# Sparse-attention scores: low query part over all 128 rows with zero-padded keys, compressed keys of both groups in one tile

## The chip, the cores and the metric

The kernel runs on one core of one Trainium2 chip. The metric is the device time of one execution in microseconds (us), the median of three runs. Engines are named as in the profile: PE is TensorE's matmul stream and PEld its weight loads, DVE is VectorE, ACT is ScalarE, POOL is GpSimd, SP issues the DMAs.

## The reference

The program is four transformer layers on 256 tokens of width 1024, all in fp32. The change is in the first, whose mixer has two halves: retention (4 heads) and sparse attention (8 query heads in 2 groups of 4, 64 wide), joined and projected. Sparse attention adds three branches with gates:

```python
s_c = einsum('bghqd,bgnd->bghqn', qb, k_cmp) * scale     # 15 compressed keys for each group
p_c = masked_softmax(s_c, cmp_end[None, :] <= t[:, None])
...
s_s = einsum('bghqd,bgqkd->bghqk', qb, kg) * scale       # chosen blocks of keys
s_w = einsum('bghqd,bgkd->bghqk', qb, kw) * scale        # a window of keys
return gb[0] * o_c + gb[1] * o_s + gb[2] * o_w
```

`k_cmp` comes from a small network over blocks of 32 tokens. With 256 tokens there are four blocks of 64 and up to eight may be chosen, and the window is 512, so both the s and the w branch see every earlier key: they are two plain causal attentions with keys of their own, ks and kw. A head j of both groups g is handled together.

## The kernel before

All weights pass through `weights` (L235): a DMA on SP brings 128x1024 fp32 into `raw`, ScalarE makes a rounded high part `hi` (L240), VectorE the rest `lo` (L243). A projection (`proj_fm`, `mm3`) makes for each of 8 slices three matmuls with 256 columns, high times high, high times low, low times high (L248 to L250). `proj_tm` (L284 to L286) does the same with 512 columns and tokens as rows. Both write PSUM banks of a pool of three, `pa`.

`even_mixer` projects in this order: the keys and values for compression, the sparse values, the queries `nq` (two pairs of tiles, L755), the keys ks and kw (L768), then the retention queries and keys rq and rk (two pairs each, L871 and L872), values rv (L873), and gates (L908). Instructions are put on the five engines in an order that is planned at build time: the program's order sets their priority, and an instruction whose operands and buffer are there can be put ahead of one that waits. On the chip each engine then works strictly in that order.

The queries: group 0 lies in rows 0 to 63, group 1 in rows 64 to 127 of `nq`. For each group a tile `qq` holds the high part of the query twice, in both halves of the rows (L762, L763), and `ql` holds the low part, group g in its own 64 rows (L764). The keys: `ksw[g]` holds the high part of ks and kw of the group in the group's own rows (L774) and the low part in the other rows (L775). The scores of head j, group g, are two matmuls, one over 128 rows (high query against high and low keys, L823) and one over the group's 64 rows (low query against high keys, L824), 512 columns for the second half of the tokens (t = 1) and 256 for the first. VectorE masks them and takes the minimum (L826), ScalarE the exponential (L833), VectorE scales (L841), PE transposes (L844 to L846), ScalarE copies (L848), and PE multiplies by the values (L861).

The compressed keys of both groups lie in `kcm`, 128 rows by 16 columns, group g in its rows (L738). Their scores are sixteen fp32 matmuls over 64 rows with 16 columns, into a bank for each group (L783). An fp32 matmul is two instructions with two weight loads in the trace. VectorE adds the mask, once for each bank (L787).

Buffers: `big` (L264) gives out tiles of 128x512 from a pool of 13. vsw, qq, ql, ksw, the three tables (L606, L869), rope (L611), the parts rqh, rql, rkh, rkl (L595), rv and rg all come from it. `rope_pair` takes a projection out of its bank: ScalarE copies with halves exchanged (L589, L590), VectorE multiplies by the two halves of rope (L592, L593) and adds (L594), in tiles of the pool `ev` (four buffers), then the split into high and low (L596, L597). At the end `out_proj` takes the four sparse heads and the four retention heads.

Of the kernel before, what the change touches and what calls it, by code (L numbers as in the profile page):

```python
# [9 lines left out]
F32 = mybir.dt.float32  # L10
F32R = mybir.dt.float32r
AF = mybir.ActivationFunctionType
ALU = mybir.AluOpType
# [155 lines left out]
def _model(es, tc, I, out):  # L169
    nc = tc.nc  # L170
    V, A, T, G = nc.vector, nc.scalar, nc.tensor, nc.gpsimd

    def pool(name, bufs, **kw):
        return es.enter_context(tc.tile_pool(name=name, bufs=bufs, **kw))

    cst = pool("cst", 1)
# [28 lines left out]
    def C(name):  # L205
        o, n = _COFF[name]
        return cs[:, o - 128:o - 128 + n]
# [50 lines left out]
    def att(tag, shape=(128, 512)):  # L258
        if tag == "sc":
            turn[0] ^= 1  # L260
            tag = f"s{turn[0]}"
        return pt.tile(list(shape), F32, tag=tag, name=tag, bufs=PB[tag])

    def big(name="b", dt=F32):  # L264
        return bp.tile([128, 2, S], dt, tag="big", name=name)
# [116 lines left out]
    def two(ap, n=2):  # L382
        return ap.unsqueeze(1).to_broadcast([128, n, S])
# [198 lines left out]
    def transpose_to(ps, src):  # L582
        T.transpose(ps, src, ident)  # L583
# [64 lines left out]
    def late_constants():  # L648
        nc.sync.dma_start(out=vg, in_=I["vec"])
        nc.sync.dma_start(out=lt, in_=I["lam"])  # L650
        V.tensor_copy(lmask, C("levmask")[:, 0:NLEV * 32].rearrange("p (l c) -> p l c", l=NLEV))
        for a in hat:
            G.memset(a, 0.0)
        le = cst.tile([128, 8], F32, name="le")
        lg = vg[:, V_LB:V_LB + 8]
        V.tensor_tensor(out=le, in0=lg, in1=lg, op=ALU.subtract)
        A.activation(le, le, AF.Exp)
        V.reciprocal(lb, le)
        V.tensor_tensor(out=lb, in0=lb, in1=le, op=ALU.mult)
        V.tensor_tensor(out=lb, in0=lb, in1=lb, op=ALU.subtract)  # L660
        V.tensor_scalar(out=lb, in0=lb, scalar1=0.0, scalar2=None, op0=ALU.max)
        V.tensor_scalar(out=om, in0=lb, scalar1=-1.0, scalar2=1.0, op0=ALU.mult, op1=ALU.add)
        for i in range(3):
            for j, o in enumerate((V_LNG, V_LNB)):
                c = vg[:, o + 8 * i:o + 8 * i + 8]
                A.activation(gbs[0][:, i, :, j], c, AF.Copy)
                V.tensor_tensor(out=gbs[1][:, i, :, j], in0=c, in1=gbs[0].bitcast(F32)[:, i, :, j], op=ALU.subtract)

    def even_mixer(X):
# [26 lines left out]
        for i in range(4):  # L696
            nc.sync.dma_start(out=w1[i], in_=I["cmpw"][:, i * 512:(i + 1) * 512])
            w1[i] = w1[i].rearrange("p (l j) -> p l j", l=8)
        nc.sync.dma_start(out=cs, in_=I["const"][:, 128:])
        vsw, gates = [], cst.tile([128, 2, 24], F32, name="gates")  # L700
        for t in range(2):
            v = big("vsw").rearrange("p a b -> p (a b)")
# [11 lines left out]
        for v in range(2):  # L714
            for a in range(2):
                n = 16 - a
                for g in range(2):
                    r = slice(64 * g, 64 * g + 64)
                    V.tensor_tensor(out=fl[v][64 * a:64 * a + 64, g, 0:n], in0=kv4[r, v, a:16],
                                    in1=pos[r, v, a].unsqueeze(1).to_broadcast([64, n, 16]), op=ALU.add)  # L720
# [4 lines left out]
        sm = lambda nm, n=32: sp.tile([128, n], F32, tag=nm, name=nm, bufs=1)  # L725
# [8 lines left out]
        pk = att("po", (128, 16))  # L734
        for g in range(2):
            T.matmul(pk[64 * g:64 * g + 64], w2[0:64], ge[0:64, 16 * g:16 * g + 16], start=True, stop=True)
        kcm = sm("kcm", 16)
        V.tensor_scalar(out=kcm, in0=pk, scalar1=0.5, scalar2=None, op0=ALU.mult)  # L738
        gx = cst.tile([128, 4, 32], F32, name="gx")
        V.tensor_scalar(out=gx[64:128], in0=ge[64:128].unsqueeze(1).to_broadcast([64, 4, 32]),  # L740
                        scalar1=0.5, scalar2=None, op0=ALU.mult)
# [4 lines left out]
                        in1=C("blk8").unsqueeze(2).to_broadcast([128, 8, 64]), op=ALU.mult)  # L746
# [3 lines left out]
        def rows(g):  # L750
            return slice(64 * g, 64 * g + 64), slice(64 - 64 * g, 128 - 64 * g)

        nq, qq, ql = [], [], []
        for p in range(2):
# [5 lines left out]
            for g in range(2):  # L760
                r, o = rows(g)
# [7 lines left out]
        k = wk.tile([128, 2, S], F32, tag="ev", name="ksw", bufs=4)  # L769
        V.tensor_tensor(out=k, in0=ps, in1=two(rb), op=ALU.mult)  # L770
        ksw = [big("ksw", F32R) for g in range(2)]
        for g in range(2):
            r, o = rows(g)
            A.activation(ksw[g][r], k[r], AF.Copy)  # L774
            V.tensor_tensor(out=ksw[g][o], in0=k[r], in1=ksw[g][r].bitcast(F32), op=ALU.subtract)  # L775

        late_constants()
        pcs = [att("sc", (128, 2, 4, 16)) for g in range(2)]
        for g in range(2):
            r = slice(64 * g, 64 * g + 64)  # L780
            for t in range(2):
                for j in range(4):
                    T.matmul(pcs[g][:, t, j], nq[j][r, t * 128:t * 128 + 128], kcm[r], start=True, stop=True)  # L783
        sc = wk.tile([128, 2, 4, 2, 16], F32, tag="csc", name="csc", bufs=1)
        cm = C("cmpmask").rearrange("p (t n) -> p t n", t=2)
        for g in range(2):
            V.tensor_tensor(out=sc[:, :, :, g], in0=pcs[g], in1=cm.unsqueeze(2).to_broadcast([128, 2, 4, 16]),  # L787
                            op=ALU.add)
        mn = sp.tile([128, 16], F32, tag="cmn", name="cmn", bufs=1)
        scv = sc.rearrange("p t j g n -> p (t j g) n")  # L790
        V.tensor_reduce(out=mn, in_=scv, axis=AX.X, op=ALU.min)
# [8 lines left out]
        for t in range(2):  # L800
            V.tensor_tensor(out=rc[:, t], in0=rc[:, t], in1=gv[:, t, 0].rearrange("p g j -> p j g"), op=ALU.mult)
        V.tensor_tensor(out=scv, in0=scv, in1=rc.rearrange("p t j g -> p (t j g)").unsqueeze(2).to_broadcast([128, 16, 16]),
                        op=ALU.mult)
# [9 lines left out]
        def nsa_heads(j):  # L813
            e = [[wk.tile([128, 384], F32, tag="e", name="e", bufs=6) for b in range(2)] for g in range(2)]
            m = [sp.tile([128, 2, 2], F32, tag="nm", name="nm", bufs=6) for g in range(2)]
            for t in (1, 0):
                n, mk = 128 + 128 * t, mask[:, 128 - 128 * t:256]
                c = slice(256 - 256 * t, 384 - 128 * t)
                for g in range(2):
                    r = rows(g)[0]  # L820
                    pp = att("sc", (128, 2, n))
                    x = slice(128 * t, 128 * t + 128)
                    T.matmul(pp, qq[j][g][:, x], ksw[g][:, :, 0:n], start=True, stop=False)  # L823
                    T.matmul(pp, ql[j][r, x], ksw[g][r, :, 0:n], start=False, stop=True)  # L824
                    for b in range(2):
                        V.tensor_tensor_reduce(out=e[g][b][:, c], in0=pp[:, b], in1=mk, scale=1.0, scalar=HUGE,  # L826
                                               op0=ALU.add, op1=ALU.min, accum_out=m[g][:, t, b:b + 1])
            pT = []
            for g in range(2):
                s = sp.tile([128, 2, 2], F32, tag="ns", name="ns", bufs=6)  # L830
                for b in range(2):
                    for t, c in ((1, slice(0, 256)), (0, slice(256, 384))):
                        A.activation(e[g][b][:, c], e[g][b][:, c], AF.Exp, scale=-1.0, bias=m[g][:, t, b:b + 1],  # L833
                                     accum_out=s[:, t, b:b + 1])
                rc = sp.tile([128, 2, 2], F32, tag="nr", name="nr", bufs=6)
                V.reciprocal(rc.rearrange("p a b -> p (a b)"), s.rearrange("p a b -> p (a b)"))
                V.tensor_tensor(out=rc, in0=rc, in1=gv[:, :, 1:3, g, j], op=ALU.mult)
                pT.append([])
                for b in range(2):
                    for t, c in ((1, slice(0, 256)), (0, slice(256, 384))):  # L840
                        V.tensor_scalar(out=e[g][b][:, c], in0=e[g][b][:, c], scalar1=rc[:, t, b:b + 1], scalar2=None,  # L841
                                        op0=ALU.mult)
                    pp = att("tr", (128, 384))
                    transpose_to(pp[:, 0:128], e[g][b][:, 256:384])  # L844
                    transpose_to(pp[:, 128:256], e[g][b][:, 0:128])
                    transpose_to(pp[:, 256:384], e[g][b][:, 128:256])  # L846
                    t = wk.tile([128, 384], F32, tag="pT", name="pT", bufs=5)
                    A.activation(t, pp, AF.Copy)  # L848
                    pT[g].append(t)
            return pT  # L850

        for j in range(4):
# [4 lines left out]
            for b in range(2):  # L857
                for v, q, c in ((0, slice(0, 256), slice(0, 256)), (1, slice(128, 256), slice(256, 384))):
                    for g in range(2):
                        cv = b * 128 + g * 64  # L860
                        T.matmul(po[64 * g:64 * g + 64, q], vsw[v][:, cv:cv + 64], pT[g][b][:, c], start=False,  # L861
                                 stop=b + v == 2, skip_group_check=True)
            if j % 2 == 0:
                hl = hpair()
            o = [x[:, j % 2, 0:S] for x in hl]
# [9 lines left out]
        for t in range(2):  # L875
# [7 lines left out]
                            in1=m.unsqueeze(2).to_broadcast([128, 4, 128]), op=ALU.subtract)  # L883
# [3 lines left out]
        for h in range(4):  # L887
            p, i = divmod(h, 2)
# [9 lines left out]
        for t in range(2):  # L898
            po = att("sc")
            for h in range(4):  # L900
                o, c = po[:, h * 128:h * 128 + 128], slice(h * 128, h * 128 + 128)
# [5 lines left out]
        for p in range(2):  # L907
# [5 lines left out]
            g = big("rg")  # L913
# [358 lines left out]
```

## Time and profile before

| | |
|---|---|
| time, median of 3 runs (lowest, highest) | 1320.19 us (1319.03, 1320.33) |
| profiled execution: span, first to last instruction | 1318.8 us |
| around the span, as the difference from the median of the runs | 1.4 us |
| busy: PE, DVE, ACT, POOL | 99%, 71%, 54%, 3% |
| mean granted TensorE clock | 0.996 |

The profiled execution is listed with its span alone; its own time with what lies around it is taken to be that of the runs. Busy is the share of the span in which an engine has at least one instruction under way. PE's instructions overlap, and their ends are modelled, so the starts of successive instructions tell more than the durations.

### The profile page before, as it was taken

The page shows a single profiled execution, that of the slowest core. Times are in us where ns is not written, and L with a number is a line of the kernel's source. Part 1 is how long each engine was busy: PE and PEld are TensorE (multiplying, and loading weights), DVE is VectorE, ACT ScalarE, POOL GpSimd, SP SyncE. Part 2 cuts the span into 40 slices and gives each one's busy share as a digit, 9 for nine tenths or more (in the row PEclk, how much of TensorE's full clock was granted, in tenths as well). Part 3 has the DMA queues.
Part 4 walks back from the last instruction along what each step waited for, and adds up shares of the span by engine and source line. Part 5 has one row for each costly group of instructions (what it writes and reads, how often), then busy time and mean ns, then how long its engine had stood idle before and what let it go on. Part 6 is the DMA issues. An engine that isn't in the chain of part 4 may idle for free.

```text
span 1318.8 us, 27456 instructions
## 1 busy us (share of the span) xinstructions
PE 1300.7 (99%) x11128; PEld 1252.1 (95%) x11128; DVE 940.3 (71%) x1753; ACT 707.1 (54%) x1180; POOL 43.2 (3%) x94
## 2 busy tenths in 40 slices
PE   8999999999999999999999999999999999999997
PEld 7978999999989899999999889999999889999997
DVE  7785764646688767465568969777679757968675
ACT  6565654444545455444458867544456656554443
POOL 0000000000000000000000111000000000000000
PEclk9999999999999999999999999999999999999998
DMA  8521665655553356555555345565555543655550
GB/s 308 178 84 57 208 203 183 190 182 156 185 183 125 117 177 189 182 189 183 155 184 180 102 145 172 164 206 168 185 168 175 167 138 124 214 187 180 180 157 33
DMA packets 65359, 219.70 MB, mean 167 GB/s; under 512 B 7504, under 2 KB 7888, under 8 KB 65232
## 3 DMA queue, kind: packets, MB, share of 16 engines
q1 hardware_dynamic: 64944, 217.82, 51.3%
q8 instruction: 88, 1.44, 0.4%
q14 instruction: 39, 0.32, 0.1%
q10 hardware_dynamic: 288, 0.12, 0.0%
HBM read 216.86 MB, written 1.05 MB: 165 GB/s over the span
## 4 chain that ended last, share of the span: by engine, by line
PE 98%; ACT 1%; DVE 1%; DMA 0%; issue 0%; POOL 0%; SPq 0%; ACTq 0%; DVEq 0%
PE pa L248 13%; PE pa L249 13%; PE pa L250 13%; PE pd L249 7%; PE pd L250 7%; PE pd L248 7%; PE s L248 4%; PE s L250 4%; PE s L249 4%; PE tr L249 3%; PE tr L248 3%; PE tr L250 3%; PE pv L284 2%; PE pv L285 2%; PE pv L286 2%; PE tr L583 1%
## 5 line engine op out<-in xcount | busy, mean ns | idle before, releaser
L240 ACT ACTIVATE hi<-raw 128x1024 fp32r<-128x1024 f32 (+2 forms) x421 | 424.4, 1017 | 496.9 <-PE pa L249 173.1
L243 DVE TENSOR_TENSOR lo<-raw,hi 128x1024 fp32r<-128x1024 f32 (+2 forms) x421 | 490.5, 1172 | 254.7 <-ACT hi L240 248.3
L249 PE MATMUL pa<-hl,hi 128*128 128x256 f32 x1424 | 403.1, 284 | 0.0
L250 PE MATMUL pa<-hh,lo 128*128 128x256 f32 x1424 | 402.7, 284 | 0.0
L248 PE MATMUL pa<-hh,hi 128*128 128x256 f32 x1424 | 401.7, 284 | 0.2 <-DVE x L479 0.2
L249 PEld LDWEIGHTS pa<-hl,hi 128*128 128x128 f32 x1424 | 269.4, 189 | 3.0 <-issue 1.0
L250 PEld LDWEIGHTS pa<-hh,lo 128*128 128x128 f32 x1424 | 269.2, 189 | 2.5 <-issue 1.5
L248 PEld LDWEIGHTS pa<-hh,hi 128*128 128x128 f32 x1424 | 267.7, 189 | 3.0 <-issue 1.1
L250 PE MATMUL pd<-hh,lo 128*128 128x258 f32 x752 | 212.7, 283 | 0.0
L249 PE MATMUL pd<-hl,hi 128*128 128x258 f32 x752 | 212.6, 283 | 0.0
L248 PE MATMUL pd<-hh,hi 128*128 128x258 f32 x752 | 210.9, 283 | 1.4 <-DVE y L543 1.4
L248 PEld LDWEIGHTS pd<-hh,hi 128*128 128x128 f32 x752 | 141.7, 190 | 1.7 <-DVE y L543 1.6
L249 PEld LDWEIGHTS pd<-hl,hi 128*128 128x128 f32 x752 | 142.5, 189 | 0.0
L250 PEld LDWEIGHTS pd<-hh,lo 128*128 128x128 f32 x752 | 142.1, 189 | 0.2
L250 PE MATMUL s<-gh,lo 128*128 128x256 f32 x352 | 98.6, 282 | 0.0
L249 PE MATMUL s<-gl,hi 128*128 128x256 f32 x352 | 98.6, 282 | 0.0
L248 PE MATMUL s<-gh,hi 128*128 128x256 f32 x352 | 96.7, 282 | 0.0
L248 PE MATMUL tr<-gh,hi 128*128 128x256 f32 x264 | 74.5, 282 | 0.0
L249 PE MATMUL tr<-gl,hi 128*128 128x256 f32 x264 | 74.5, 282 | 0.0
L250 PE MATMUL tr<-gh,lo 128*128 128x256 f32 x264 | 74.5, 282 | 0.0
L250 PEld LDWEIGHTS s<-gh,lo 128*128 128x128 f32 x352 | 66.5, 189 | 0.0
L249 PEld LDWEIGHTS s<-gl,hi 128*128 128x128 f32 x352 | 66.4, 189 | 0.0
(350 smaller groups left out, 1917.6 us busy)
## 6 DMA issues: line engine op xcount, KB each, us to landing
raw<-w SPq DMA_DIRECT2D x120, 512.0 KB, 3.6
raw<-v SPq DMA_DIRECT2D x120, 512.0 KB, 4.0
raw<-w_e SPq DMA_DIRECT2D x19, 512.0 KB, 5.3
raw<-w_aqk SPq DMA_DIRECT2D x16, 512.0 KB, 3.7
raw<-w SPq DMA_DIRECT2D x16, 384.0 KB, 3.1
raw<-v SPq DMA_DIRECT2D x16, 384.0 KB, 3.1
raw<-w_of SPq DMA_DIRECT2D x8, 512.0 KB, 3.3
raw<-w_oq SPq DMA_DIRECT2D x8, 512.0 KB, 4.4
```

The source lines that it names most:

```text
L240: A.activation(hi, raw, AF.Copy)
L243: V.tensor_tensor(out=lo, in0=raw, in1=hi.bitcast(F32), op=ALU.subtract)
L248: T.matmul(ps, a, h[0], start=first, stop=False, skip_group_check=True)
L249: T.matmul(ps, a, h[1], start=False, stop=False, skip_group_check=True)
L250: T.matmul(ps, b, h[0], start=False, stop=last, skip_group_check=True)
L284: T.matmul(ps[t], xh, a, start=k == 0, stop=False)
L285: T.matmul(ps[t], xh, b, start=False, stop=False)
L286: T.matmul(ps[t], xl, a, start=False, stop=k == 7)
L583: T.transpose(ps, src, ident)
```

## The change

The low query part of L824 is multiplied over all 128 rows instead of over the group's 64: a new tile `kz[g]` holds a copy of the group's high keys in the group's rows and zeros in the others, so that the other group's rows of `ql` add nothing. This needs two more tiles of the pool `big`, a memset of half a tile on GpSimd and a copy of half a tile on ScalarE for each group.

The compressed keys go into `kbd`, 128 rows by 2x16 columns, zero outside the two diagonal blocks, cleared by GpSimd and filled by two VectorE instructions. The scores of both groups are then one matmul over 128 rows with 32 columns, eight matmuls in all, into one bank, and the mask is added in one VectorE instruction.

```diff
+        kbd = cst.tile([128, 2, 16], F32, name="kbd")
+        G.memset(kbd, 0.0)
...
-        kcm = sm("kcm", 16)
-        V.tensor_scalar(out=kcm, in0=pk, scalar1=0.5, scalar2=None, op0=ALU.mult)
+        for g in range(2):
+            r = slice(64 * g, 64 * g + 64)
+            V.tensor_scalar(out=kbd[r, g], in0=pk[r], scalar1=0.5, scalar2=None, op0=ALU.mult)
...
         ksw = [big("ksw", F32R) for g in range(2)]
+        kz = [big("kz", F32R) for g in range(2)]
         for g in range(2):
             r, o = rows(g)
+            G.memset(kz[g].bitcast(F32)[o], 0.0)
+            A.activation(kz[g][r], k[r], AF.Copy)
             A.activation(ksw[g][r], k[r], AF.Copy)
             V.tensor_tensor(out=ksw[g][o], in0=k[r], in1=ksw[g][r].bitcast(F32), op=ALU.subtract)
...
-        pcs = [att("sc", (128, 2, 4, 16)) for g in range(2)]
-        for g in range(2):
-            r = slice(64 * g, 64 * g + 64)
-            for t in range(2):
-                for j in range(4):
-                    T.matmul(pcs[g][:, t, j], nq[j][r, t * 128:t * 128 + 128], kcm[r], start=True, stop=True)
+        pcs = att("sc", (128, 2, 4, 32))
+        for t in range(2):
+            for j in range(4):
+                T.matmul(pcs[:, t, j], nq[j][:, t * 128:t * 128 + 128], kbd.rearrange("p g n -> p (g n)"),
+                         start=True, stop=True)
...
-        for g in range(2):
-            V.tensor_tensor(out=sc[:, :, :, g], in0=pcs[g], in1=cm.unsqueeze(2).to_broadcast([128, 2, 4, 16]),
-                            op=ALU.add)
+        V.tensor_tensor(out=sc.rearrange("p t j g n -> p t (j g) n"),
+                        in0=pcs.rearrange("p t j (g n) -> p t (j g) n", g=2),
+                        in1=cm.unsqueeze(2).to_broadcast([128, 2, 8, 16]), op=ALU.add)
...
-                    r = rows(g)[0]
                     pp = att("sc", (128, 2, n))
                     x = slice(128 * t, 128 * t + 128)
                     T.matmul(pp, qq[j][g][:, x], ksw[g][:, :, 0:n], start=True, stop=False)
-                    T.matmul(pp, ql[j][r, x], ksw[g][r, :, 0:n], start=False, stop=True)
+                    T.matmul(pp, ql[j][:, x], kz[g][:, :, 0:n], start=False, stop=True)
```

## Rows read from the trace of the kernel before

**Rows 1.** The page, busy time by engine (us, share of span, instructions).
```profile
PE 1300.7 (99%) x11128; PEld 1252.1 (95%) x11128; DVE 940.3 (71%) x1753; ACT 707.1 (54%) x1180; POOL 43.2 (3%) x94
```

**Rows 2.** Windows: stretch, length, busy us by engine, granted clock, DMA.
```profile
56.00:66.00 10.00, 10.00 (x67) 8.24 (x66) 7.10 (x29) 7.39 (x22) 0.00 (x0) 1.00 0.42 125
66.00:76.00 10.00, 10.00 (x68) 8.39 (x69) 9.67 (x31) 7.03 (x19) 0.00 (x0) 1.00 0.35 104
```

**Rows 3.** Timeline of PE around two score pairs: start, duration, instruction.
```profile
54.98 0.39 PE L823 MATMUL s<-ksw,qq 128*128 128x512 f32 x1
...
55.95 0.28 PE L249 MATMUL pa<-hl,hi 128*128 128x256 f32 x1
...
108.89 0.28 PE L823 MATMUL s<-ksw,qq 128*128 128x256 f32 x1
109.10 0.38 PE L824 MATMUL s<-ksw,ql 64*128 64x256 f32 x1
109.41 0.39 PE L249 MATMUL pa<-hl,hi 128*128 128x256 f32 x1
109.63 0.28 PE L602 MATMUL s<-rqh,rkh 128*128 128x256 f32 x1
109.63 0.19 PEld L602 LDWEIGHTS s<-rql,rkh 128*128 128x128 f32 x1
109.75 0.28 PE L602 MATMUL s<-rql,rkh 128*128 128x256 f32 x1
```

**Rows 4.** Timeline of PE: the compressed scores, and narrow fp32 matmuls elsewhere.
```profile
48.15 2.43 PE L783 MATMUL s<-kcm,nq 64*128 64x16 f32 x24
50.51 0.38 PE L248 MATMUL pa<-hh,hi 128*128 128x256 f32 x1
...
1306.32 0.58 PE L333 MATMUL s<-ncol,x 128*128 128x1 f32 x4
1306.77 0.58 PE L333 MATMUL s<-mcol,acc 128*128 128x1 f32 x4
```

**Rows 5.** Timeline of PE, and windows with the granted clock before the DMA columns.
```profile
51.33 0.40 PE L248 MATMUL pa<-hh,hi 128*128 128x256 f32 x1
...
54.73 0.29 PE L249 MATMUL pa<-hl,hi 128*128 128x256 f32 x1
...
51.50:54.50 3.00, 3.00 (x16) 3.00 (x15) 2.25 (x6) 2.31 (x3) 0.00 (x0) 0.50 0.54 182
...
162.41 1.03 PE L333 MATMUL po<-mcol,sq 128*128 128x1 f32 x8
...
160.00:168.00 8.00, 8.00 (x70) 8.00 (x69) 2.84 (x4) 3.07 (x3) 1.85 (x2) 1.00 0.27 81
```

**Rows 6.** A GpSimd group (count, busy, mean ns); timeline of ScalarE.
```profile
L653 POOL MEMSET hat<- 128x768 f32 x3 | 2.1, 737 | 0.3 <-POOLq L1263 0.3
...
50.87 0.63 ACT L763 ACTIVATE qq<-nq 64x512 fp32r<-64x512 f32 x1
51.52 1.28 ACT L774 ACTIVATE ksw<-ksw 64x512 fp32r<-64x512 f32 x2
```

**Rows 7.** Timelines of all engines: idle time and its releaser in brackets.
```profile
48.30 1.70 SPq L606 DMA_DIRECT2D tab<-tables  x3
...
60.08 0.59 ACT L590 ACTIVATE sw<-pa 64x512 f32<-64x512 f32 x1
...
69.45 0.38 PE L824 MATMUL s<-ksw,ql 64*128 64x256 f32 x1
...
69.56 0.69 DVE L611 TENSOR_TENSOR rope<-tab,rb 128x512 f32<-128x512 f32 x1
...
76.60 0.38 PE L824 MATMUL s<-ksw,ql 64*128 64x256 f32 x1
76.91 0.39 PE L248 MATMUL pa<-hh,hi 128*128 128x256 f32 x1
...
104.59 0.63 ACT L596 ACTIVATE rkh<-c 128x512 fp32r<-128x512 f32 x1 [0.43 <-PE s L823]
```

## The prediction

> **What bounds the kernel now.** I read the page first: TensorE (PE) has work in 99% of the 1318.8 us, VectorE (DVE) 71%, ScalarE (ACT) 54%, GpSimd (POOL) 3% [rows 1]. Busy shares of a pipelined engine prove little, so I went to the stage that the change touches, from about 45 to 140 us, by stretches: PE is busy without a gap although VectorE reaches 9.67 of 10 us [rows 2]. Then the timeline of PE there: the score matmuls of the sparse heads are single pairs inside long runs of projection matmuls (rq, rk, rv, rgate), which have no tie to the heads' softmax chains and fill every wait. Whatever PE need not do in this stage therefore comes off the end, as long as such filling work is at hand. That condition is the whole risk, so last I read what the filling work itself waits for: buffers.
>
> **Part 1, the low query part over 128 rows.** Sixteen L824 matmuls leave the 64-row form. In a plain stretch 256-column matmuls start 0.12 us apart, each with weights of its own. Around an L824 that is not so: from the start of an L823 with 256 columns to the start of the second instruction behind the L824 it takes 109.63 - 108.89 = 0.74 us, where three such steps would take 0.36; the loss is 0.38. With 512 columns it takes 55.95 - 54.98 = 0.97; at the same rate per column (an estimate from the 0.12) this would be 0.24 + 0.24 + 0.12 = 0.60, the loss 0.37. About a quarter of the loss lies before the L824 (0.21 instead of 0.12), the rest behind it (0.31 and 0.22), so I read it as the price of going into the 64-row form and out again [rows 3]. 8 x 0.38 + 8 x 0.37 = 6.0 us. The new matmul reads as many columns and loads as many weight columns, and 64 of its 128 key rows are zeros, which costs nothing that these rows show. Bounds: 0 if the loss belongs to something that stays (a rival below), 6.0 if all goes. I take 6.0, since L602 chains three matmuls with three different weights over 128 rows at 0.12 [rows 3], which is what L823 and the new line will be.
>
> One rule of the Trainium skill speaks against this part. "TensorE: Matmul & The Clock Gate", section Part 3 (What overlaps and what doesn't), says that a weight load overlaps running matmuls only where its row group differs; by that, giving up the 64-row groups would gain nothing, and the sum below would lack the 6.0. The rows disagree for this kernel: the load of L602's second matmul lasts 0.19 us, starts with the first matmul at 109.63, and its own matmul still starts at 109.75 [rows 3].
>
> **Part 2, the compressed scores.** Sixteen fp32 matmuls appear in the trace as 32 instructions of 64 rows and 16 columns. 24 of them take 50.51 - 48.15 = 2.36 us, 0.098 each, so 32 take 3.15 [rows 4]. Eight matmuls are left, 16 instructions of 128 rows and 32 columns. No row shows this form; the nearest are fp32 with 128 rows and one column, four in 1306.77 - 1306.32 = 0.45 us, 0.11 each [rows 4]. Bounds 0.098 (the load as it is with 64 rows) and 0.12 (a full 256-column step). I take 0.11: 1.8 us, so 1.35 saved (1.2 to 1.6). The two visits to the 64-row form go too; each costs between nothing and the 0.38 of part 1, I take 0.3 for both.
>
> **Part 3, the clock.** Right behind that run of narrow matmuls the granted clock is at 0.50, its lower level of 1.2 GHz, from 51.33 to 54.73, 16 steps of 0.21 instead of 0.12 us [rows 5]: 1.5 us lost. It was at full speed before. The new run has 1.8 us of narrow matmuls at most instead of 2.4, with twice the columns and rows in each. A run of eight one-column instructions, 0.9 us between full ones, is followed by no fall: that stretch is granted 1.00 [rows 5]. The new run lies between the two, in parts perhaps, as the old one (8 and 24). Bounds 0 and 1.5; I take 1.5 and give the fall that stays a case of its own.
>
> **Part 4, what is added.** GpSimd clears kbd and two halves of kz; a memset larger than these takes 0.74 us [rows 6], and GpSimd is idle for 97% of the span: nothing, and if that cover were gone, 1.5 us before the first score. VectorE writes kbd in two small instructions instead of one and the masked scores in one instead of two: nothing either way. ScalarE copies k into kz twice, 64x512 each as the ksw copies are, two in 1.28 us [rows 6], and this lies where ScalarE is full: it works from qq straight into ksw until 52.80 [rows 6]. The first score needs kz and ksw of group 0, so 51.52 + 1.28 + 0.69 for VectorE's subtraction = 53.5. PE would arrive 1.35 + 0.3 + 1.5 = 3.15 earlier than the 54.98 of now, at 51.8. The 1.7 us between are covered by projections of rq, which PE has in plenty there; without them they would be lost, so 0 to 1.7, and I take 0. Behind the copies on ScalarE stand the next weight split (L240) and the exponentials; they shift by 1.3 us.
>
> **Part 5, the buffers.** kz takes two of the 13 "big" buffers. By the code the heads hold ten (vsw 2, qq 4, ql 2, ksw 2), and the three tables, loaded from 48.30, make 13. The trace shows that this pool already binds: ScalarE's half of the rotary step of rq is done at 60.67, but rope itself is made only at 69.56, right behind the L824 at 69.45 that lets go of part of qq; rkh at 104.59 waits for a score matmul in the same way [rows 7]. With kz there are 15 for 13. Two tables stand ahead of rope in the program, so I expect rope to get not the first buffer that head 1 frees but the third, behind the last score of head 1 (76.60 in the trace). PE by then has put rq0, rq1 and rk0 into its three accumulator banks, and needs one back for rk1, which starts at 76.91, just there [rows 7]. It then waits for rope and the product that empties the bank, two VectorE instructions of 0.69 [rows 7] with hand-overs: some 1.4 to 2 us, if the heads offer nothing in between. Later rql and rqh miss buffers until head 3's scores, and rgate's bank comes late by about the same. Together 0 (the order is planned so that rope goes first) to 4 us. I take 2, as the first wait is forced by counting and the second has other work beside it.
>
> **The sum.** 6.0 + 1.35 + 0.3 + 1.5 = 9.15 saved, 2 given back: 7.1. The profiled execution has 1318.8 us of span, so 1311.7; the median of the runs is 1320.2, 1.4 above that span, so **1313** for the measured time.
>
> **The rivals.**
> - *The clock falls all the same.* For it: what counts is not known, and the new run is still narrow. Against: it is shorter and denser. Costs 1.5: 1314.6, from 1312.6 to 1316.6.
> - *The 0.38 is a load that isn't hidden and stays.* For it: the weight load before L824 starts only with its matmul. Against: L602. Then 6.0 is missing: 9.15 - 6.0 - 2 = 1.1 saved, 1319. (This is what the Trainium skill's rule on overlap, cited in part 1, would give; the trace speaks against it.)
> - *Longer waits for buffers.* The planned order lays the projections so that PE stands for 5 to 9 us in several places: 1316 to 1320. For it: 15 for 13, and the "ev" buffers that hold the rotary results until rqh and rql exist number only four. Against: in the trace rql waits and PE does not.
> - *Slower: rope comes only with head 3.* If the buffers of head 1 go to the tables and to others, rope waits from 76.60 to the release just ahead of 104.59 [rows 7]. All three banks are then full, and what PE did in that time beside the heads, 48 steps for rk1 (5.8 us) and 48 twice as long for rv (11.3 us, estimated from the 0.12), slides behind: 17 us lost, 9.15 saved, so 1328. It decides from 9.2 us of standing PE on. For it: the count. Against: rope stands ahead of all of rq and rk in the program, and three buffers come free with head 1.
>
> **The chances.** Forecast (1311 to 1315) 0.58; clock falls 0.12; load stays 0.08; longer waits 0.08; slower 0.14. A measurement of this kernel tells about 0.2% (2.6 us) from no change. Faster: 0.58 + 0.12 + half of the longer waits 0.04 = 0.74; same: 0.08 + 0.04 = 0.12; slower 0.14. The range runs from 1310 (no wait for buffers, and part 2 at its better bound) to 1319.5, which takes in the stalls and the load that stays, and leaves out mainly the slower case: 0.15. The forecast's own range is 1311 to 1315.
>
> **What would show it.** In the new profile: L823 and the ql matmul followed by their successors at 0.12 or 0.24 with no step of 0.31 (part 1); 16 instructions for the compressed scores in under 2 us (part 2); granted clock 1.00 between 48 and 56 us (part 3); the kz copies on ScalarE just ahead of ksw, and PE busy with projections meanwhile (part 4); PE idle for a moment between head 1's last score and rk1, waiting for VectorE, rope made later than one head's scores after the tables, and the second and third tables loaded long after the first (part 5). The forecast is wrong if PE stands for more than 5 us between 60 and 110 us, or if the matmuls behind the ql line still start late.

## The result, and the profile after

The changed kernel takes 1310.76 us (median of 4 runs, 1310.16 to 1311.18) against 1319.61 (4 runs, 1318.50 to 1320.33) beside it: ratio 0.9932, 95% interval 0.9920 to 0.9945. The forecast was 1313, range 1310 to 1319.5. The profiled execution has a span of 1309.0 us, 9.8 less than before. One execution of a kernel below, sp_only, is left out: it took 1392.6 us at a mean granted clock of 0.849.

The page, busy time by engine: nothing but TensorE has moved by more than 1.1 us [rows 1].

```profile
PE 1289.9 (99%) x11112; PEld 1246.4 (95%) x11112; DVE 939.7 (72%) x1753; ACT 708.2 (54%) x1182; POOL 44.3 (3%) x97
```

The compressed scores of before came in two parts; [rows 4] has the second, and this is the first:

```profile
45.62 0.63 PE L783 MATMUL s<-kcm,nq 64*128 64x16 f32 x8 [0.23 <-DVE nq L757]
46.18 0.39 PE L248 MATMUL pa<-hh,hi 128*128 128x256 f32 x1
```

The timeline of PE after: the compressed scores, then one score pair of 512 columns, one of 256, and the place where PE stood.

```profile
45.92 0.63 PE L787 MATMUL s<-kbd,nq 128*128 128x32 f32 x4 [0.35 <-DVE nq L760]
46.39 0.37 PE L248 MATMUL pa<-hh,hi 128*128 128x256 f32 x1
...
48.73 1.42 PE L787 MATMUL s<-kbd,nq 128*128 128x32 f32 x12
49.99 0.36 PE L249 MATMUL pa<-hl,hi 128*128 128x256 f32 x1
...
54.96 0.40 PE L827 MATMUL s<-ksw,qq 128*128 128x512 f32 x1
55.20 0.40 PE L828 MATMUL s<-kz,ql 128*128 128x512 f32 x1
55.44 0.28 PE L248 MATMUL pa<-hh,hi 128*128 128x256 f32 x1
55.56 0.28 PE L249 MATMUL pa<-hl,hi 128*128 128x256 f32 x1
...
67.88 0.28 PE L827 MATMUL s<-ksw,qq 128*128 128x256 f32 x1
68.00 0.28 PE L828 MATMUL s<-kz,ql 128*128 128x256 f32 x1
68.12 0.28 PE L248 MATMUL pa<-hh,hi 128*128 128x256 f32 x1
...
71.31 0.47 PE L827 MATMUL s<-ksw,qq 128*128 128x512 f32 x1 [0.23 <-DVE nm L830]
...
73.73 0.36 PE L827 MATMUL s<-ksw,qq 128*128 128x256 f32 x1 [0.28 <-DVE nr L840]
...
74.31 0.38 PE L248 MATMUL pa<-hh,hi 128*128 128x256 f32 x1
```

A pair with the matmul behind it now takes 0.24 + 0.24 + 0.12, or three times 0.12: no step of these two pairs is stretched, as it was in [rows 3]. The reckoning of part 1 can be made at all sixteen pairs (steps of the pair and of the matmul behind it, less 0.12 for each 256 columns). It gives 6.7 us lost before and 1.2 after, most of that where PE stands. The compressed scores take 46.39 - 45.92 = 0.47 and 49.99 - 48.73 = 1.26 us for 16 instructions, 0.108 each [rows 4].

Windows after (stretch, length, busy us by engine, granted clock, DMA): the clock stays at 1.00, its upper level of 2.4 GHz, where it was at 0.50 for 3.4 us [rows 5], and PE stands for 0.6 us between 66 and 76, where it had no gap [rows 2]. The timeline above has two of these waits, 0.23 and 0.28, for VectorE instructions of the heads' softmax; the last 0.1 lies just ahead of 74.31.

```profile
46.00:56.00 10.00, 10.00 (x83) 9.91 (x84) 8.51 (x14) 9.77 (x16) 0.00 (x0) 1.00 0.33 117
56.00:66.00 10.00, 10.00 (x81) 9.74 (x80) 9.93 (x42) 9.15 (x26) 0.00 (x0) 1.00 0.70 197
66.00:76.00 10.00, 9.38 (x68) 7.38 (x68) 7.91 (x27) 7.99 (x26) 0.00 (x0) 1.00 0.48 147
```

Timelines of the queue and of the other engines after: the tables come one early and two late, where all three came at 48.30; rope follows at 71.08 instead of 69.56 [rows 7]. The kz copies lie among the ksw copies.

```profile
33.33 1.19 POOL L778 MEMSET kz<- 64x512 f32 x2 [14.61 <-PE po L726]
48.60 0.83 SPq L606 DMA_DIRECT2D tab<-tables  x1
51.71 0.63 ACT L779 ACTIVATE kz<-ksw 64x512 fp32r<-64x512 f32 x1
52.25 0.62 ACT L780 ACTIVATE ksw<-ksw 64x512 fp32r<-64x512 f32 x1
...
68.19 2.66 SPq L606 DMA_DIRECT2D tab<-tables  x2
...
71.08 0.69 DVE L611 TENSOR_TENSOR rope<-tab,rb 128x512 f32<-128x512 f32 x1
...
73.59 0.66 DVE L592 TENSOR_TENSOR c<-pa,rope 128x512 f32<-128x512 f32 x1
```

One thing was not in the forecast. The same matmul can be found in both traces, counted from the end (from 175 us on both have the same matmuls in the same order), and its two start times subtracted. The changed kernel is 8.1 us ahead at 175.24 (time of before), where its edits lie behind it; at 1306.77 [rows 4] it is 9.9 ahead. The lines are the matmul at 175.24 in the trace of before and of after, then the one at 1306.77 in the trace of after:

```profile
175.24 0.28 PE L249 MATMUL pa<-hl,hi 128*128 128x256 f32 x1
...
167.10 0.28 PE L249 MATMUL pa<-hl,hi 128*128 128x256 f32 x1
...
1296.88 0.58 PE L333 MATMUL s<-mcol,acc 128*128 128x1 f32 x4
```

So 1.8 us are gained in matmuls that no line of the diff touches. A window of a feed-forward layer shows them, before and then after: 506 matmuls in 60 us where there were 502, PE busy throughout and at full clock in both.

```profile
1196.00:1256.00 60.00, 60.00 (x502) 60.00 (x501) 43.01 (x76) 26.81 (x34) 0.00 (x0) 1.00 0.57 182
...
1196.00:1256.00 60.00, 60.00 (x506) 60.00 (x505) 42.73 (x73) 27.31 (x35) 0.00 (x0) 1.00 0.58 183
```

### The profile page after: what moved, and what is told of

It is laid out like the page before. It is cut to its first block, busy times and chain, and to the rows that moved or that the text cites. A ratio compares the mean times of both kernels' runs of the same rounds, so it can differ in the third digit from the quotient of the medians.

```text
span 1309.0 us, 27435 instructions
## 1 busy us (share of the span) xinstructions
PE 1289.9 (99%) x11112; PEld 1246.4 (95%) x11112; DVE 939.7 (72%) x1753; ACT 708.2 (54%) x1182; POOL 44.3 (3%) x97
## 4 chain that ended last, share of the span: by engine, by line
PE 96%; DMA 1%; DVE 1%; ACT 1%; issue 0%; SPq 0%; POOL 0%; ACTq 0%; DVEq 0%
PE pa L249 13%; PE pa L248 13%; PE pa L250 13%; PE pd L249 7%; PE pd L248 7%; PE pd L250 7%; PE s L248 4%; PE s L250 4%; PE s L249 4%; PE tr L248 3%; PE tr L249 3%; PE tr L250 3%; PE pv L284 2%; PE pv L285 2%; PE pv L286 2%; PE tr L583 1%
```

## The experiments

Each ratio is against runs of the kernel before on the same chip (medians 1320.4 to 1320.7; 1319.61 beside the changed kernel). "Clock" is the granted clock of 50 to 56 us, "PE" its busy time of 66 to 76 us; "at 175" and "at 1307" are how far the matmuls that start at 175.24 and 1306.77 us in the trace of before have moved; the last column counts matmuls from 1196 to 1256 us (502 before).

| kernel | median, us (range) | ratio (95%) | clock | PE | at 175 | at 1307 | count |
|---|---|---|---|---|---|---|---|
| changed | 1310.76 (1310.16-1311.18) | 0.9932 (0.9920-0.9945) | 1.00 | 9.38 | -8.1 | -9.9 | 506 |
| p1_only | 1313.16 (1312.42-1313.73) | 0.9945 (0.9930-0.9960) | 0.72 | 10.00 | -6.9 | -6.9 | 503 |
| p2_only | 1315.80 (1315.39-1316.28) | 0.9967 (0.9954-0.9979) | 1.00 | 10.00 | -3.2 | -5.3 | 506 |
| no_kz | 1309.89 (1309.39-1310.06) | 0.9920 (0.9905-0.9935) | 1.00 | 10.00 | -9.4 | -11.5 | 505 |
| kz_acc | 1310.45 (1310.10-1310.77) | 0.9925 (0.9910-0.9939) | 1.00 | 10.00 | -8.5 | -10.5 | 505 |
| narrow2 | 1312.29 (1311.54-1313.67) | 0.9941 (0.9926-0.9955) | 1.00 | 10.00 | -7.3 | -9.4 | 506 |
| before11 | 1319.62 (1318.48-1320.44) | 0.9994 (0.9984-1.0003) | 1.00 | 10.00 | -1.9 | -1.9 | 502 |
| twice64 | 1323.24 (1320.85-1323.74) | 1.0020 (1.0011-1.0030) | 0.72 | 10.00 | +2.1 | +2.2 | 503 |
| moved | 1318.13 (1316.49-1318.65) | 0.9978 (0.9967-0.9989) | 0.72 | 10.00 | -0.1 | -2.3 | 505 |
| cst_only | 1320.74 (1319.06-1321.32) | 1.0001 (0.9990-1.0011) | 0.72 | 10.00 | +0.4 | +0.4 | 502 |
| sp_only | 1317.93 (one run) | - | 0.72 | 10.00 | -0.3 | -2.7 | 506 |
| acc_pad64 | 1310.21 (1309.98-1310.93) | 0.9927 (0.9910-0.9943) | 1.00 | 10.00 | -8.6 | -10.4 | 505 |
| after_sp64 | 1312.80 (1312.51-1313.04) | 0.9944 (0.9928-0.9961) | 1.00 | 9.39 | -8.4 | -8.1 | 502 |

**Each part alone.** p1_only is the kernel before with kz and its matmul, and nothing of the compressed scores; p2_only is the changed kernel with the old ql matmul and without kz:

```diff
 p1_only (beside the kernel before)
+        kz = [big("kz", F32R) for g in range(2)]
...
+            G.memset(kz[g].bitcast(F32)[o], 0.0)
+            A.activation(kz[g][r], k[r], AF.Copy)
...
-                    T.matmul(pp, ql[j][r, x], ksw[g][r, :, 0:n], start=False, stop=True)
+                    T.matmul(pp, ql[j][:, x], kz[g][:, :, 0:n], start=False, stop=True)
 p2_only (beside the changed kernel): these lines the other way round
```

> Part 1 alone (kz and the low query part over 128 rows; the compressed scores stay 32 narrow instructions over 64 rows). Theory A (every step that PE saves comes off the end, and the clock fall belongs to the narrow run): steps of 0.12 and 0.24 behind the low part, 6.0 us saved, about 0.5 given back to waits for buffers, the granted clock still at 0.50 for some 3 us behind the narrow run: 5 to 6 us under before, ratio 0.9955 to 0.9965. Rival B (the fall was a matter of the 64-row score pairs that follow): no fall, 7 us under before, ratio 0.9945.

> Part 2 alone (block-diagonal compressed keys; the low query part stays over 64 rows). Theory A: 1.2 us of narrow instructions and 1.5 us of clock saved, 2.7 under before, ratio 0.998; the pairs still lose 0.38 each. Rival B: the fall stays, 1.2 under before, ratio 0.999.

p1_only is 6.9 us ahead at 175 and stays there to the end; its clock falls as before. p2_only is 3.2 ahead at 175 with no fall, and 5.3 at the end. The fall thus goes with part 2, and so does the late gain. The medians of the two, 7.4 and 4.8 under before, add up to 12.2, more than what both together gain (the changed kernel's median is 9.8 under the same 1320.6). The 7.4 is a little high: p1_only's median lies between two runs at 1312.4 and 1312.7 (mean clock 0.997) and two at 1313.6 and 1313.7 (0.995). The traces at 175 say the same, 6.9 + 3.2 = 10.1 against 8.1. The next experiments are about what is lost (PE standing) and what is not the work of the edits at all.

**What kz costs.** no_kz takes ql over 128 rows against ksw itself; the low part of the other group's queries is then multiplied with this group's key remainders and added, which changes the computation. kz_acc keeps kz in other slots:

```diff
 no_kz (and no kz tiles, memsets and copies)
-                    T.matmul(pp, ql[j][:, x], kz[g][:, :, 0:n], start=False, stop=True)
+                    T.matmul(pp, ql[j][:, x], ksw[g][:, :, 0:n], start=False, stop=True)
 kz_acc
-        kz = [big("kz", F32R) for g in range(2)]
+        kz = [sp.tile([128, 2, S], F32R, tag="acc", name="kz") for g in range(2)]
```

> The changed kernel without kz: the low query part is multiplied over 128 rows with ksw itself, so the other group's low query times the low keys is added to the scores (this changes the computation). No third use of buffers, no copies, no memsets. Theory A: PE's sum without anything given back, 8.7 to 9.2 under before, at most 0.6 better than the changed kernel; the three tables load together and rope comes with the first buffer. Rival C (buffers and copies hold back 2 us or more that other luck covers): 2 us or more better than the changed kernel, ratio under 0.9925.

> The changed kernel with kz in two buffers of another pool that lies idle in this stage (the accumulators of the norm statistics), so that the pool of 13 has its two tiles back; copies and memsets stay. Theory A: as without kz, 8.7 to 9.2 under before, PE without standing between 60 and 110 us. If the copies on ScalarE cost something by themselves, it is slower than the run without kz by that.

Without kz the trace is 1.2 us further ahead at 175, the median 0.9 lower. With kz kept out of the big buffers, the three tables come together again, rope is made at 68.19 and PE stands nowhere between 66 and 76:

```profile
48.62 1.83 SPq L606 DMA_DIRECT2D tab<-tables  x3
...
68.19 0.69 DVE L611 TENSOR_TENSOR rope<-tab,rb 128x512 f32<-128x512 f32 x1
```

That is worth 0.35 us at 175 and 0.3 in the medians, whose ranges overlap. By the expectation's last sentence the copies have a price all the same: kz_acc has them and PE never stands between 46 and 130 us, yet it is 0.9 us behind no_kz at 175 and 0.6 in the medians, whose ranges do not overlap. The orders of work differ too, so that it is the copies themselves is not shown.

**Two buffers fewer, alone.** before11 is the kernel before with a smaller pool.

```diff
-    bp, wk = pool("bp", 13), pool("wk", 2)
+    bp, wk = pool("bp", 11), pool("wk", 2)
```

> The kernel before with 11 big buffers in place of 13: as many as the changed kernel leaves to the others once the two kz tiles have theirs; nothing else is changed. Theory A (the prediction's part 5): the rope tables' later parts wait for buffers, TensorE stands about where it stood in the changed kernel, 0.5 us and at most 4: ratio 1.0004, up to 1.003. Theory B, the buffers cost nothing where the kz copies and memsets are not there (it is these on ScalarE, GpSimd and VectorE that made TensorE stand): ratio 1.000, TensorE busy for all of 66 to 76 us.

Theory B: rope comes at 74.28, later than in the changed kernel, and PE has no gap. (Of the 1.9 us at 175, 1.5 are the fall of the clock that this trace lacks, as said below.) Missing buffers alone cost nothing as long as the planned order still has projections for PE; narrow2, with the buffers of the changed kernel, has no gap either (10.00). The 0.6 us of the changed kernel are thus a matter of its one order of work, not a price of 15 tiles in 13 slots. The surprise stands in the clock column: the trace shows no fall, behind the very run of 64-row matmuls that is followed by one in the kernel before.

```profile
74.28 0.69 DVE L611 TENSOR_TENSOR rope<-tab,rb 128x512 f32<-128x512 f32 x1
...
48.04 2.43 PE L783 MATMUL s<-kcm,nq 64*128 64x16 f32 x24
50.39 0.38 PE L248 MATMUL pa<-hh,hi 128*128 128x256 f32 x1
...
50.00:56.00 6.00, 6.00 (x41) 4.99 (x41) 4.80 (x11) 4.08 (x7) 0.00 (x0) 1.00 0.21 78
```

**A longer run of the new form.** narrow2 issues the eight block-diagonal matmuls twice.

```diff
-        for t in range(2):
-            for j in range(4):
+        for t, j in [(t, j) for i in range(2) for t in range(2) for j in range(4)]:
+            if True:
```

> The changed kernel with the eight matmuls of the compressed scores issued twice: 16 of 128x32 become 32 instructions (the trace counts two for each float32 matmul), as many on TensorE as in the kernel before; the result is the same. The run of narrow matmuls lasts 16 x 0.108 = 1.7 us longer, 3.5 us against the 2.9 us of the kernel before. Theory A, it is the length of the run of short matmuls that lets the granted clock fall to 0.50: it falls here again, for about 3.4 us behind the run, and that costs the 1.5 us of the prediction too: 3.2 us over the changed kernel, 1314.0 us. Theory B, it was the 64 rows and the 16 columns (a quarter of the array's rows times columns): the clock stays at 1.00, 1.7 us over, 1312.5 us. On the drift of 1.9 us after 175 us: if the place of the tiles makes it, it stays; if the number of instructions makes it, another 1.9 us is lost.

Theory B: no fall in the trace, although the run is longer than the old one (its 28 instructions of the second part are busy for 3.21 us, the 24 of before for 2.43 [rows 4]).

```profile
48.64 3.21 PE L787 MATMUL s<-kbd,nq 128*128 128x32 f32 x28
...
50.00:56.00 6.00, 6.00 (x51) 5.92 (x51) 4.15 (x7) 5.12 (x9) 0.00 (x0) 1.00 0.24 95
```

The median is 1.5 us over the changed kernel, 1.7 were expected; the trace is 0.9 behind at 175, with the 0.6 of standing PE gone. Of its four executions one took 1313.67 at a mean clock of 0.995, the others 1311.5 to 1312.3 at 0.996; whether the clock fell in that one, no trace shows. The late gain stays, so it is not the number of instructions.

**The 64-row matmul twice in a row** (kernel before; the low part counts twice, which changes the computation).

```diff
+                    T.matmul(pp, ql[j][r, x], ksw[g][r, :, 0:n], start=False, stop=False)
                     T.matmul(pp, ql[j][r, x], ksw[g][r, :, 0:n], start=False, stop=True)
```

> The kernel before with each low-part matmul over 64 rows issued twice in a row, into the same accumulation: the low part of the scores counts twice, which changes the computation. Theory A (the prediction's): what costs is the way into and out of the 64-row form, and that is paid once for a pair of them; the second costs a plain step, 8 x 0.24 + 8 x 0.12 = 2.9 us, ratio 1.0022. Theory B (the rival of the load that isn't hidden): each 64-row matmul pays for its own load, so the second costs about what the first does, 8 x (0.24 + 0.38) + 8 x (0.12 + 0.37) = 8.9 us, or with one of its two ends alone, 8 x (0.24 + 0.19) + 8 x (0.12 + 0.19) = 5.9 us; ratio 1.0045 to 1.0067.

Theory A: +2.5 us in the median, +2.1 to 2.2 in the trace. In its timeline of PE

```profile
54.84 0.40 PE L823 MATMUL s<-ksw,qq 128*128 128x512 f32 x1
55.16 0.50 PE L824 MATMUL s<-ksw,ql 64*128 64x512 f32 x1
55.50 0.39 PE L825 MATMUL s<-ksw,ql 64*128 64x512 f32 x1
55.82 0.39 PE L248 MATMUL pa<-hh,hi 128*128 128x256 f32 x1
56.05 0.28 PE L249 MATMUL pa<-hl,hi 128*128 128x256 f32 x1
...
55.16 0.18 PEld L824 LDWEIGHTS s<-ksw,ql 64*128 64x128 f32 x1 [0.25 <-issue]
55.27 0.19 PEld L825 LDWEIGHTS s<-ksw,ql 64*128 64x128 f32 x1
```

it is 56.05 - 54.84 = 1.21 us from the first to the second instruction behind, 0.24 more than the 0.97 of [rows 3], a plain step of 512 columns for a second 64-row matmul. The same reckoning gives a loss of 0.36 to 0.49 us at fifteen of the sixteen visits (the last is interleaved with another pair), as for one matmul in the kernel before. The loss belongs to the change of form, and not to each load of weights. The weight loads (the last two lines) say the same: behind a 128-row matmul the load for L824 starts only with its own matmul, behind a 64-row one the load for L825 starts 0.23 us ahead of it.

**The late gain: a matter of place.** Part 2 moves tiles: kbd adds 128 bytes of a partition to the constants, and kcm takes its 64 out of the small pool. Behind these lie the weights' and activations' pools, the small pool, then the big buffers and the work pool. Four kernels move tiles alone, with no instruction added: moved does both with the matmuls of before, cst_only and sp_only do one each, and acc_pad64 shifts all pools of kz_acc by 64 bytes.

```diff
 moved
+        kbd = cst.tile([128, 2, 16], F32, name="kbd")
-        kcm = sm("kcm", 16)
+        kcm = kbd[:, 0]
 cst_only
+        pad = cst.tile([128, 32], F32, name="pad")
 sp_only
-        kcm = sm("kcm", 16)
+        kcm = sm("gu0")[:, 0:16]
 acc_pad64 (beside kz_acc)
+        pad = cst.tile([128, 16], F32, name="pad")
 after_sp64 (beside the changed kernel)
+        pad = sm("pad", 16)
```

> The kernel before with one tile moved: kcm (the compressed keys, 64 bytes of a partition) lies in a tile of 128 bytes among the constants, where the changed kernel has its block-diagonal tile, and no longer in the small pool. No instruction is added or taken away. Four kernels with part 2 gained another 1.9 to 2.1 us after 175 us, in matmuls that no edit touches (steps of 0.118 in place of 0.120 us between 1196 and 1260 us); the kernel with part 1 alone gained nothing there. Theory A, the place of the tiles in memory: what lies behind the constants is shifted as in the changed kernel, and this one gains 1.9 to 2.1 us over its length with the same order of work, span 1316.7 to 1316.9, ratio 0.9985. Theory B, the sixteen instructions fewer on TensorE: nothing is gained, span 1318.8, ratio 1.000.

> The kernel before with an unused tile of 128 bytes of a partition among the constants, where the changed kernel has its block-diagonal tile: every pool behind the constants lies 128 bytes further on; the compressed keys stay in the small pool; no instruction is added. The kernel with that tile and without the 64 bytes of the compressed keys in the small pool gained 2.3 us between 165 and 1307 us with the order of work of the kernel before. Theory A, it is the shift of the weights' and activations' pools by 128 bytes: the same 2.3 us here. Theory B, it is the 64 bytes by which the big buffers and the work pool, which lie behind the small pool, stand otherwise (128 forward in this kernel and 64 forward in that one): no gain here, within 0.2 us of the kernel before up to the last matmul.

> The kernel before with the compressed keys in the slot of another small tile that is dead by then: the small pool is 64 bytes of a partition shorter, the big buffers and the work pool behind it lie 64 bytes nearer, and the constants, the weights' and the activations' pools stay where they are. Theory A (the shift of the weights' and activations' pools makes the gain): nothing is gained between 165 and 1307 us. Theory B (an odd number of 64-byte steps for the big buffers and the work pool makes it): 2.3 us are gained as in the kernel with the moved tile.

> The changed kernel with its kz tiles in the two accumulator slots of the small pool (1310.45 us when it ran as it stands) and with 64 bytes of a partition left unused among the constants, so that all pools behind them lie 64 bytes further on. No instruction is added. If places decide by odd or even steps of 64 bytes, the gain in the later matmuls turns: either it is lost again (1312.5 us), or another place is better still (below 1309.5 us). If 64 bytes make no difference: 1310.5 us, within 0.3.

moved gains 2.1 us between 175 and 1307 with the work of before. cst_only gains nothing there, sp_only 2.4 (one trace). So it is the 64 bytes that leave the small pool. That odd or even steps of 64 bytes decide, as the second half of theory B had it, falls with acc_pad64: 64 bytes for all pools alike change nothing (the late gain is 1.8 there, 2.0 in kz_acc). What fits all of them, though no run singles it out, is that it counts how far tiles behind kcm's place lie from tiles ahead of it. The last kernel gives the changed one those 64 bytes back:

> The changed kernel with an unused tile of 64 bytes of a partition in the small pool, at the place that the compressed keys had in the kernel before: the tiles behind it lie as far from the weights' and activations' pools as in the kernel before. No instruction is added. The trace of the changed kernel gained 1.7 us between 165 and 1307 us in matmuls that no edit touches. Theory A, that gain comes of the 64 bytes that the small pool lost: here it is gone, the distance to the kernel before stays what it is at 165 us (8.2 us) up to the last matmul, the time is 1312.5 us (the changed kernel ran in 1310.8), ratio 0.9938. Theory B, it comes of something else in the change: 1310.8 us, ratio 0.9925, and the distance grows to 9.9 us as in the changed kernel.

Theory A: the trace is 8.4 us ahead at 175 and 8.1 at the end, the count is back at 502, and the median is 2.0 us above the changed kernel.

```profile
1196.00:1256.00 60.00, 60.00 (x502) 60.00 (x501) 42.24 (x74) 26.71 (x34) 0.00 (x0) 1.00 0.58 182
...
1298.71 0.58 PE L333 MATMUL s<-mcol,acc 128*128 128x1 f32 x4
```

## Why the prediction was right

1. **Part 1** held, and was sized a little low. The stretched steps are gone at ten of the sixteen pairs (0.24 and 0.12); the other six stand where PE waits or right behind transposes or value products. twice64 and p1_only settle the rival of the load that isn't hidden: the loss is one of going into and out of the 64-row form. Alone the part is worth 6.9 us in the trace, 0.43 for each of 16 matmuls; the two pairs of [rows 3] gave 0.375. Of the 0.9 above the forecast 0.4 lie in the steps of the pairs: all sixteen lose 6.7 before and 0.3 in p1_only, as six visits right behind transposes, value products or another score pair lose 0.44 to 0.56, the other ten 0.37 to 0.38. The other 0.5 was not traced to single steps. What the Trainium skill states fits this ("TensorEngine Tiling (Array Packing)", Key Properties: a change of tiling mode drains TensorE); the traces show the stretched steps and not the drain itself, and 0.4 us a visit is their price in this kernel. The Trainium skill's rule on overlap that spoke against this part ("TensorE: Matmul & The Clock Gate", Part 3, What overlaps and what doesn't) does not hold for these traces: every matmul of a pair has 128 rows and weights of its own, and with 256 columns they start 0.12 us apart.
2. **Part 2**: 2.92 us (0.56 and 2.36) have become 0.47 + 1.26 = 1.73, so 1.2 saved, not 1.35; an instruction is at 0.108, forecast 0.11. The 0.3 for going in and out did not come: the steps behind the old and the new run are alike (0.22 and 0.20). PE waits 0.35 us for `nq` ahead of the first part, 0.23 before, which takes back 0.1.
3. **Part 3**: the fall is gone in the trace of the changed kernel, 1.5 us. In seven traces with the wide form there is no fall; in seven with the 64-row run there are six. Executions without a trace fit this: of 23 runs of the kernel before in one series, 5 took 1318.8 to 1319.5 us at a mean clock of 0.997 and 18 took 1320.2 to 1321.4 at 0.995 or 0.996 (9 of 29 at 0.997 in the other three series). That the clock did not fall in the quicker ones is inferred from these times; the mean clock alone does not tell it, as 0.996 stands over traces with the fall (before) and without it (the changed kernel). So the run makes the fall likely and not certain, and the step was right for most executions and not for each. narrow2 shows that a longer run of 128 rows and 32 columns is followed by none in its trace; which of the two sizes matters stays open.
4. **Part 4** cost no gap: the copies delay ksw (the last copy ends at 54.03), and PE has projections until the first score at 54.96, with 10.00 of 10 us busy. The 1.7 us of the bound are not seen as a wait. But the part was put at nothing and is not shown to be nothing: the trace of no_kz, which has neither copies, memsets nor buffers for kz, is 1.2 us ahead at 175, and that of kz_acc, with copies and memsets and no standing, lies 0.9 behind no_kz. PE is busy from 46 to 130 us in both, so these are mostly longer steps and not waits; which ones stays open.
5. **Part 5** had the sequence right and the price too high. Tables late, rope made behind the last score of head 1 (70.13 in the trace after), PE standing just ahead of rk1 at 74.31 came as said; but the rows put it at 0.6 us instead of 2. The assumption that the heads offer nothing in between failed: between rope at 71.08 and the first product at 73.59 PE ran scores and value products of the heads, and 0.5 of the 0.6 were waits of those scores. One reading was loose: in the kernel before, VectorE was in another instruction until 69.48, so rope's wait for its buffer at 69.56 [rows 7] was 0.08 us there, and it is L823 and not L824 that reads qq. kz_acc and before11 show that neither the copies nor the missing buffers alone make PE stand, and narrow2 that both together need not.
6. **The sum.** By the steps of the trace the pairs give 6.7 - 1.2 = 5.5 (two of the three waits of PE lie within them), the compressed scores 1.2 and the clock 1.5; less 0.3 for the third wait and 0.1 for the longer wait for `nq` this is 7.8. The changed kernel is 8.1 ahead at 175 us, so 0.3 is not traced. The forecast was 7.1. The other 1.8 us to 9.9 come from a term that the prediction lacked, the place of the tiles: after_sp64, without it, runs in 1312.8, where the forecast said 1313. That agreement is partly luck: a part 1 sized a little low and a part 4 put at nothing offset a part 5 priced too high. The measured 1310.8 lies within the range, near its lower end, and for a reason that the range was not made for.

## What to carry to other kernels

A matmul over 64 rows between matmuls over 128 costs its neighbours 0.4 us here; zero-padding it to 128 rows cost at most 1.2 us in all (no_kz against the changed kernel) for 6 to 7 gained, and it pays once for each visit, not for each matmul. Before a gain of one or two us in a thousand is put down to an edit, compare the same instructions far behind it in both traces: what moves there is not the edit's work, and a tile of the same size put back at the old place shows how much. Where a stage has work without ties to fill waits, a scarce buffer delayed its owner and not the end (before11); the price is set by what else the engine can run at that moment, not by the length of the wait.

## What the runs showed of the hardware that was not expected

- Taking 64 bytes of a partition out from between two groups of tiles made matmuls with no other change quicker: 506 in 60 us where there were 502, 1.8 to 2.4 us over the kernel. The mean step of that window is 0.1186 us instead of 0.1195. Which two tiles are concerned, and why, stays open. The Trainium skill ("SBUF — State Buffer", section SBUF: two separate sides) says that TensorE waits for no other engine's access to that memory, which no run here tests.
- The granted clock behind the same run of 64-row fp32 matmuls, 2.4 us long, fell to 0.50 in six traces and stayed at 1.00 in a seventh (before11), and the run times of the kernel before lie in two groups 1.7 us apart, which fit it. What else decides was not found.
- 16 fp32 instructions of 128 rows and 32 columns take 0.108 us each, 32 of 64 rows and 16 columns 0.091 (2.92 us): twice the rows and columns for a fifth more time.
